# Decoder layer, float32 weights split into two float32r parts: low parts of the second-product and embedding weights by an accumulating DMA instead of a VectorE subtraction

## The chip, the cores and the metric

One Trainium2 chip, one core of it. The metric is device time in microseconds of one execution. PE is TensorE (matmuls), DVE is VectorE, ACT is ScalarE, POOL is GpSimd, SP is SyncE, which here only issues DMAs. POOL and ACT can issue DMAs too.

## What is computed

One decoder layer on 512 tokens of width 1024, in float32:

```
x = LN1(alpha*x + 0.5*SwiGLU_1(x))              # (silu(x @ Wg) * (x @ Wu)) @ W2, inner width 2816
h = x @ W_in                                    # gated delta rule (4 heads) and differential attention (4 heads)
x = LN2(alpha*x + concat(y_A, y_B) @ W_out)
x = LN3(alpha*x + 0.5*SwiGLU_2(x) + sigmoid(x @ W_pg) * (p @ W_pp))
```

## The kernel before

Precision. A product of float32 accuracy is made of three matmuls in the faster type float32r: each operand is split into a high part (the value cast to float32r) and a low part (the value minus its high part), and `mm3` (L185 to L189) adds high x high, high x low and low x high into one PSUM tile. So every weight tile that arrives from HBM goes through a split: `split` (L149) has ACT cast the raw tile to the high part `wh` and then DVE subtract it from the raw tile, which gives the low part `wl`.

Tiles. A weight unit is a tile of 128 partitions x 1024 float32 (512 KB). `load` (L153) takes a raw buffer out of a ring of four, has SP load it, and splits it. Two kinds of weights pass through it. The first kind (`ahead`, `take`) are the first-product, mixer, output and gate weights; they are read in order out of `in_wa_dram` through a ring of four `wh`/`wl` pairs. The second kind (`side`, L180) are the second-product weights of the two SwiGLU stages (W2, 22 tiles of 128 x 1024 in each) and the two tiles of W_pp, 46 tiles in all, read from `in_wb_dram`. The W2 tiles have a ring of six pairs (`w2p`).

Stages. `first_ffn`, then `mixers`, then `second_ffn`. A SwiGLU stage (`ffn`, L240) goes through the inner width in groups of 4, 6, 6 and 6 blocks of 128 columns. For each block, 24 matmuls per factor make the gate and the up factor in PSUM; `glu` has ACT apply silu, DVE multiply by the up factor, ACT cast the result to `hh` and DVE subtract to `hl`. At the end of a group come its second products: for each of four token tiles and two halves, all blocks of the group are accumulated into one PSUM tile `pb`, with the W2 tiles `wh`, `wl` as the moving operand. In the first group of `first_ffn` the four blocks are computed together, with k outermost, so that all four `glu` and all four side tiles come at once, just ahead of the second products; in every other group a block takes 48 matmuls, and its side tile comes with it.

Order. Each engine has a queue that runs in order. The order is not that of the source: when the kernel is built, a scheduler places the instructions of all engines, by costs of its own, and the ring buffers are given out in the order that it finds. So an edit can move instructions that it doesn't name. A wait on a semaphore holds up all that is queued behind it on the same engine.

Of the kernel before, what the change touches and what calls it, by code (L numbers as in the profile page):

```python
# [8 lines left out]
F32 = mybir.dt.float32  # L9
F32R = mybir.dt.float32r  # L10
BF16 = mybir.dt.bfloat16
AF = mybir.ActivationFunctionType
ALU = mybir.AluOpType
# [3 lines left out]
P = 128  # L17
# [30 lines left out]
WIDE = 2 * (512 + 2 * H)  # L48
# [32 lines left out]
class Lane:  # L81
    """A chain of steps; each step says how long it holds the tensor engine and when the next one can follow."""

# [24 lines left out]
class Layer:  # L108
# [38 lines left out]

    # ---------------------------------------------------------------- weights
    def split(self, hi, lo, src):  # L149
        self.nc.scalar.copy(hi, src)  # L150
        self.nc.vector.tensor_tensor(lo, src, hi.bitcast(F32), ALU.subtract)  # L151
# [28 lines left out]
    def side(self, pool, tag):  # L180
        r = self.load(pool, tag, self.wb[self.nb])
        self.nb += 1
        return r

# [5 lines left out]

    # ---------------------------------------------------------------- layer norm of one token tile
    def norm_natural(self, t, eps, gbt, store=None, cut=768, cuts=(0, 512, 1024)):
# [45 lines left out]

    # ---------------------------------------------------------------- SwiGLU
    def ffn(self, zone, k_outer, evac_first, natural, turn):  # L240
# [65 lines left out]

    # ---------------------------------------------------------------- start: constants and the first inputs
    def first_ffn(self):
# [75 lines left out]

    # ---------------------------------------------------------------- per-layer embedding, second SwiGLU
    def second_ffn(self):
# [63 lines left out]

    # ---------------------------------------------------------------- token mixers, output projection, LN 2
    def mixers(self):
        with ExitStack() as zone:
            self.mix_zone(zone)

    def mix_zone(self, zone):
        tc, nc = self.tc, self.nc
        act, dve, pool, pe = nc.scalar, nc.vector, nc.gpsimd, nc.tensor
# [46 lines left out]

        # ------------------------------------------------------------ projections
        def block(t, w, pq, k0, k1):
# [180 lines left out]

        # ------------------------------------------------------------ delta rule inside a chunk
        def lv4(l):  # L690
            return bc(self.LVM[:, l * P:(l + 1) * P], 1, H)
# [55 lines left out]
        def diagonal():  # L747
            """Inverts the 16 x 16 diagonal blocks of all chunks and heads, a block on each partition."""
            for b in range(8):
                r = slice(b * 16, b * 16 + 16)  # L750
# [19 lines left out]
            for b in range(8):  # L770
                r = slice(b * 16, b * 16 + 16)
# [6 lines left out]

        # ------------------------------------------------------------ attention of one query tile and head
        def attention(t, h):  # L780
# [41 lines left out]

        # ------------------------------------------------------------ delta rule over the chunks
        def to_mix(y, t, k0, tag):
# [68 lines left out]

        # ------------------------------------------------------------ output projection
        def project_out(w, half, t):
# [36 lines left out]

        # ------------------------------------------------------------ order of the work
        values_and_gates()
# [10 lines left out]
        heads = [(t, h) for t in range(NT) for h in range(H)]  # L945
# [118 lines left out]
```

## Time and profile before

| | |
|---|---|
| time, median of 3 runs | 1130.65 us (1130.26 to 1130.72) |
| span of the profiled execution, first to last instruction | 1128.3 us |
| PE busy | 1112.6 us, 99% |
| DVE busy | 521.7 us, 46% |
| ACT busy | 367.9 us, 33% |
| POOL busy | 113.7 us, 10% |
| DMA, mean over the span | 94 GB/s, 105.76 MB |

The profile is of one execution; of that execution the page prints the span but no time of its own, so the 2.35 us between its span and the median of the three runs are taken as what lies around a span. Busy time of PE counts matmuls that overlap, so that one lasts some 0.39 us in the rows and the next starts some 0.23 us after it. Times in the rows are from the start of the span.

### The profile page before, as it was taken

The numbers are of one execution on the slowest core, as the hardware profiler recorded it, in microseconds if no ns is written. First come the engines' busy times: TensorE is split into PE (matmuls) and PEld (weight loads), VectorE is DVE, ScalarE is ACT, GpSimd is POOL, SyncE is SP. The second block draws the span as 40 slices with busy tenths as digits, with TensorE's granted clock in tenths as the row PEclk, the third lists the DMA queues.
The fourth block names the chain that finished last, engine by engine and source line by source line (L and its number), as shares of the span: only waits on it lengthen the run. The fifth ranks groups of instructions, "written<-read, shape, count | busy, mean of one in ns | idle before, by whom it ended". The sixth has DMA issues, their size and how long they took to land.

```text
span 1128.3 us, 13157 instructions
## 1 busy us (share of the span) xinstructions
PE 1112.6 (99%) x5193; PEld 900.3 (80%) x5193; DVE 521.7 (46%) x822; ACT 367.9 (33%) x642; POOL 113.7 (10%) x189
## 2 busy tenths in 40 slices
PE   9999999999999999999999999999999999999996
PEld 7788888888888978778866888888888888888885
DVE  4534423432435365457674669364333324423435
ACT  4513303320331266324376533433123213303300
POOL 2000000000002202432101204000000000000013
PEclk9999999999999999999999999999999999999998
DMA  9624402420340042023110222534224214302202
GB/s 344 208 73 143 137 19 94 150 94 23 131 154 30 1 130 76 30 84 85 57 56 1 75 75 76 168 104 129 84 94 149 75 38 149 132 19 94 94 1 75
DMA packets 38062, 105.76 MB, mean 94 GB/s; under 512 B 10160, under 2 KB 12096, under 8 KB 38000
## 3 DMA queue, kind: packets, MB, share of 16 engines
q1 hardware_dynamic: 31776, 96.71, 25.8%
q0 software_dynamic: 1808, 6.04, 1.5%
q10 hardware_dynamic: 4416, 2.16, 0.7%
q8 instruction: 41, 0.67, 0.2%
q14 instruction: 21, 0.17, 0.0%
HBM read 102.41 MB, written 2.49 MB: 93 GB/s over the span
## 4 chain that ended last, share of the span: by engine, by line
PE 96%; ACT 1%; DVE 1%; POOL 1%; issue 1%; DMA 0%; POOLq 0%; SPq 0%; ACTq 0%; DVEq 0%
PE pb L187 14%; PE pb L189 14%; PE pb L188 14%; PE pc L187 7%; PE pc L188 7%; PE pc L189 7%; PE pa L188 7%; PE pa L187 7%; PE pa L189 7%; PE pc L792 2%; PE pa L725 1%; PE pa L504 1%; PE pc L811 1%; PE pa L731 1%; PE pa L229 1%
## 5 line engine op out<-in xcount | busy, mean ns | idle before, releaser
L150 ACT CAST wh<-raw 128x1024 fp32r<-128x1024 f32 (+2 forms) x181 | 183.1, 1034 | 479.4 <-PE pc L188 149.3
L151 DVE TENSOR_TENSOR wl<-raw,wh 128x1024 fp32r<-128x1024 f32 (+2 forms) x181 | 215.2, 1210 | 176.8 <-ACT wh L150 172.8
L187 PE MATMUL pb<-wh,hh 128*128 128x512 f32 (+1 forms) x358 | 138.5, 387 | 0.0
L188 PE MATMUL pb<-wl,hh 128*128 128x512 f32 (+1 forms) x358 | 138.2, 386 | 0.0
L189 PE MATMUL pb<-wh,hl 128*128 128x512 f32 (+1 forms) x358 | 138.1, 386 | 0.0
L188 PE MATMUL pa<-XL,wh 128*128 128x512 f32 x344 | 136.4, 396 | 0.0
L188 PE MATMUL pc<-XL,wh 128*128 128x512 f32 x344 | 136.2, 396 | 0.0
L187 PE MATMUL pc<-XH,wh 128*128 128x512 f32 x344 | 136.2, 396 | 0.0
L189 PE MATMUL pc<-XH,wl 128*128 128x512 f32 x344 | 136.1, 396 | 0.0
L187 PE MATMUL pa<-XH,wh 128*128 128x512 f32 x344 | 136.0, 395 | 0.1
L189 PE MATMUL pa<-XH,wl 128*128 128x512 f32 x344 | 135.6, 394 | 0.0
L187 PE MATMUL pb<-wh,XH 128*128 128x512 f32 (+2 forms) x288 | 111.0, 386 | 0.7 <-DVE RES L908 0.5
L188 PE MATMUL pb<-wl,XH 128*128 128x512 f32 (+2 forms) x288 | 107.3, 372 | 0.2 <-DVE wl L151 0.2
L189 PE MATMUL pb<-wh,XL 128*128 128x512 f32 (+2 forms) x288 | 107.2, 372 | 0.0
L250 DVE TENSOR_TENSOR sg<-sg,pc 128x512 f32<-128x512 f32 x43 | 29.5, 687 | 151.1 <-PE pc L189 150.4
L301 DVE TENSOR_TENSOR RES<-RES,pb 128x512 f32<-128x512 f32 (+1 forms) x49 | 33.1, 676 | 114.7 <-PE pb L189 114.7
L203 POOL TENSOR_SCALAR bnrs<-bnmv 128x1 f32<-128x1 f32 x12 | 6.0, 498 | 745.9 <-DVE bnmv L201 745.9
L187 PEld LDWEIGHTS pb<-wh,hh 128*128 128x128 f32 x358 | 67.3, 188 | 14.1 <-ACT hh L150 0.3
L189 PEld LDWEIGHTS pb<-wh,hl 128*128 128x128 f32 x358 | 67.3, 188 | 13.6
L188 PEld LDWEIGHTS pb<-wl,hh 128*128 128x128 f32 x358 | 67.3, 188 | 13.5
L187 PEld LDWEIGHTS pa<-XH,wh 128*128 128x128 f32 x344 | 64.6, 188 | 16.6 <-ACT wh L150 0.8
L187 PEld LDWEIGHTS pc<-XH,wh 128*128 128x128 f32 x344 | 64.7, 188 | 15.8
(233 smaller groups left out, 1483.3 us busy)
## 6 DMA issues: line engine op xcount, KB each, us to landing
raw<-in_wa_dram SPq DMA_DIRECT2D x127, 512.0 KB, 3.6
raw<-in_wb_dram SPq DMA_DIRECT2D x46, 512.0 KB, 3.5
raw<-in_wd_dram SPq DMA_DIRECT2D x4, 520.0 KB, 4.0
RES<-in_xn_dram POOLq DMA_DIRECT2D x4, 512.0 KB, 11.2
gb<-in_gb_dram POOLq DMA_DIRECT2D x8, 256.0 KB, 4.6
xr<-in_xT_dram ACTq DMA_DIRECT2D x7, 256.0 KB, 5.2
TT<-in_gb_dram POOLq DMA_DIRECT2D x4, 256.0 KB, 3.4
out_dram<-RES SPq DMA_DIRECT2D x4, 256.0 KB, 2.1
```

The source lines that it names most:

```text
L150: self.nc.scalar.copy(hi, src)
L151: self.nc.vector.tensor_tensor(lo, src, hi.bitcast(F32), ALU.subtract)
L187: pe.matmul(o, wh, xh, start=first, stop=False)
L188: pe.matmul(o, wh, xl, start=False, stop=False)
L189: pe.matmul(o, wl, xh, start=False, stop=last)
L229: self.nc.tensor.transpose(pt[:, q * P:(q + 1) * P], self.RES[t][:, c:c + P], self.ident)
L250: dve.tensor_tensor(s, s, pu, ALU.mult)
L301: dve.tensor_tensor(rj, rj, pd, ALU.add)
L504: pe.transpose(dst[:, h * P:(h + 1) * P], src[:, h, :], ident)
L725: pe.matmul(pt[:, h * P:(h + 1) * P], MP[:, 0, c, h, :], TT[:, c, h, :], start=True, stop=True)
L731: pe.matmul(pt[:, h * P:(h + 1) * P], UU[:, c, h, :], qq[:, h * P:(h + 1) * P], start=True, stop=True)
L792: pe.matmul(sc[m], DQT[r, h, t * P:(t + 1) * P], DKT[r, h, 0:n], start=True, stop=False)
```

## The change

`side` no longer goes through `load` and `split`. For each of its 46 tiles, SP still loads the raw tile and ACT still casts it to the high part. Then ACT writes minus the high part into the low tile, and POOL issues a DMA that adds the weights, read once more from HBM, onto that tile. DVE has no part in it. `load` and `split` themselves are unchanged for all other weights and activations. The rest of the diff removes comments and moves line numbers down by 8.

```
     def side(self, pool, tag):
-        r = self.load(pool, tag, self.wb[self.nb])
+        nc = self.nc
+        src = self.wb[self.nb]
+        r = self.rawp.tile([P, WIDE], F32, name=self.nm("raw"), tag="raw")[:, 0:1024]
+        hi = pool.tile([P, 1024], F32R, name=self.nm("wh"), tag=tag + "h")
+        lo = pool.tile([P, 1024], F32R, name=self.nm("wl"), tag=tag + "l")
+        nc.sync.dma_start(r, src)
+        nc.scalar.copy(hi, r)
+        nc.scalar.activation(lo, hi.bitcast(F32), AF.Copy, scale=-1.0)
+        nc.gpsimd.dma_start(lo, src, accum_op=ALU.add)
         self.nb += 1
-        return r
+        return hi, lo
```

What this moves, in the first group of `first_ffn`. The four side tiles there are, in the program before, `wh_476`/`wl_477`, `wh_482`/`wl_483`, `wh_488`/`wl_489` and `wh_494`/`wl_495`, and in the changed program `wh_476`/`wl_477`, `wh_483`/`wl_484`, `wh_490`/`wl_491` and `wh_497`/`wl_498`; they are called side tiles 0 to 3 below. `wh_410` and `wh_442` are units of the first kind; `sg`, `hh`, `hl` belong to the four `glu`.

First place: ACT, from side tile 1 to the last cast of the four `glu`. Before:

```order
L150 CAST wh_482<-raw_481 128x1024 [waits DMAHW0_49]
L150 CAST hh_450<-sg_447 128x512 [waits DVE_49]
L150 CAST hh_457<-sg_454 128x512 [waits DVE_49]
L150 CAST wh_488<-raw_487 128x1024 [waits DMAHW1_49]
L150 CAST wh_442<-raw_441 128x1024 [waits DMAHW6_49,PE_49,Activation_49]
L249 ACTIVATE sg_461<-pa_163 128x512 [waits DVE_49]
L249 ACTIVATE sg_468<-pb_165 128x512 [waits DVE_49]
L150 CAST wh_494<-raw_493 128x1024 [waits DMAHW2_49]
L150 CAST hh_464<-sg_461 128x512 [waits DVE_49]
L150 CAST hh_471<-sg_468 128x512 [waits DVE_49]
```

The same place on ACT in the changed program, from the low part of side tile 1 to that of side tile 3:

```order
L188 ACTIVATE wl_484<-wh_483 128x1024 [waits Activation_49]
L150 CAST hh_450<-sg_447 128x512 [waits DVE_49]
L150 CAST wh_442<-raw_441 128x1024 [waits DMAHW6_49,PE_49]
L150 CAST hh_457<-sg_454 128x512 [waits DVE_49]
L257 ACTIVATE sg_461<-pa_163 128x512 [waits DVE_49]
L187 CAST wh_490<-raw_489 128x1024 [waits DMAHW1_49]
L257 ACTIVATE sg_468<-pb_165 128x512 [waits DVE_49]
L188 ACTIVATE wl_491<-wh_490 128x1024 [waits Activation_49]
L150 CAST hh_464<-sg_461 128x512 [waits DVE_49]
L150 CAST hh_471<-sg_468 128x512 [waits DVE_49]
L187 CAST wh_497<-raw_496 128x1024 [waits DMAHW2_49]
L188 ACTIVATE wl_498<-wh_497 128x1024 [waits Activation_49]
```

The negated copies stand in the queue between the casts, and the cast of side tile 3 (`wh_494` before, `wh_497` now) has moved behind the last two `hh`. Ahead of this piece ACT now has, in this order, the cast `wh_476`, its negated copy, the cast `wh_483`, the cast `wh_410`, the load of the silu table and the silus `sg_447` and `sg_454`; before, these were `wh_476`, `wh_410`, the table and the two silus, and `wh_482` came behind them.

Second place: PE, the start of the second products of that group. `pb_499` before and `pb_503` now is the first half of the first token tile, `pb_513` and `pb_517` its second half, and `pa_625` and `pa_629` are the gate factor of the next block. Before, after 12 matmuls into `pa_625`:

```order
L187 MATMUL pb_499<-wh_476,hh_450 128x512 [waits Activation_49]
L188 MATMUL pb_499<-wl_477,hh_450 128x512 [waits DVE_49]
L189 MATMUL pb_499<-wh_476,hl_451 128x512 [waits DVE_49]
L187 MATMUL pb_499<-wh_482,hh_457 128x512
L188 MATMUL pb_499<-wl_483,hh_457 128x512
L189 MATMUL pb_499<-wh_482,hl_458 128x512 [waits DVE_49]
L187 MATMUL pa_625<-XH,wh_344 128x512
L188 MATMUL pa_625<-XL,wh_344 128x512
L189 MATMUL pa_625<-XH,wl_345 128x512
L187 MATMUL pa_625<-XH,wh_344 128x512
L187 MATMUL pb_499<-wh_488,hh_464 128x512 [waits Activation_49]
L188 MATMUL pb_499<-wl_489,hh_464 128x512 [waits DVE_49]
```

The same place on PE in the changed program, after 16 matmuls into `pa_629`:

```order
L195 MATMUL pb_503<-wh_476,hh_450 128x512 [waits Activation_49]
L196 MATMUL pb_503<-wl_477,hh_450 128x512 [waits DMASW5_49]
L197 MATMUL pb_503<-wh_476,hl_451 128x512 [waits DVE_49]
L195 MATMUL pb_503<-wh_483,hh_457 128x512
L196 MATMUL pb_503<-wl_484,hh_457 128x512 [waits DMASW6_49]
L197 MATMUL pb_503<-wh_483,hl_458 128x512 [waits DVE_49]
L195 MATMUL pb_517<-wh_476,hh_450 128x512 [waits DVE_49]
L195 MATMUL pb_503<-wh_490,hh_464 128x512 [waits Activation_49]
L196 MATMUL pb_517<-wl_477,hh_450 128x512
L197 MATMUL pb_517<-wh_476,hl_451 128x512
L195 MATMUL pb_517<-wh_483,hh_457 128x512
L196 MATMUL pb_517<-wl_484,hh_457 128x512
```

The group's second products start four matmuls later, the low parts are now waited for on DMA semaphores (DMASW), and the first use of side tile 2's low part has moved from the 12th matmul of the piece to the 21st, behind two more into `pb_517` and six more into `pa_629`.

Third place: PE, around the first use of side tile 3's low part. `pc_660` is the up factor of the next block. In the program before, the low part `wl_495` was first used as the 20th matmul from the start of the second products:

```order
L189 MATMUL pb_499<-wh_488,hl_465 128x512 [waits DVE_49]
L187 MATMUL pb_499<-wh_494,hh_471 128x512 [waits Activation_49]
L188 MATMUL pb_499<-wl_495,hh_471 128x512
L189 MATMUL pb_499<-wh_494,hl_472 128x512 [waits DVE_49]
L189 MATMUL pb_513<-wh_482,hl_458 128x512
```

In the changed program the same use, of `wl_498`, is the 34th, with these rows ahead of it:

```order
L195 MATMUL pb_503<-wh_497,hh_471 128x512 [waits Activation_49]
L196 MATMUL pb_517<-wl_491,hh_464 128x512
L197 MATMUL pb_517<-wh_490,hl_465 128x512
L195 MATMUL pb_517<-wh_497,hh_471 128x512
L196 MATMUL pa_629<-XL,wh_344 128x512
L197 MATMUL pa_629<-XH,wl_345 128x512
L195 MATMUL pc_660<-XH,wh_378 128x512
L196 MATMUL pc_660<-XL,wh_378 128x512
L197 MATMUL pc_660<-XH,wl_379 128x512
L195 MATMUL pc_660<-XH,wh_378 128x512
L196 MATMUL pc_660<-XL,wh_378 128x512
L196 MATMUL pb_503<-wl_498,hh_471 128x512 [waits DMASW0_49]
```

Of the 33 matmuls between the first of the second products and this one, 20 go into `pb` and 13 into `pa` and `pc`. Behind the group's second products PE has that much less of `pa` and `pc` left; from there on its order is that of before, but for one matmul that changes places with its neighbours in the first group of `second_ffn`.

Two more things follow from the rings. On SP, the raw load of side tile 1 (`raw_482`) is now given the raw buffer of side tile 0, and that of side tile 3 (`raw_496`) the buffer of side tile 1, so each waits for the ACT cast of that tile; before, they waited for subtractions of units of the first kind. On POOL, the accumulating DMAs stand behind the constant and LN 1 loads at the start, and in each stage all of them stand ahead of the stage's first layer-norm instruction.

## Rows read from the trace of the kernel before

**Rows 1.** The page: span, and busy time of PE (share, instructions).

```profile
span 1128.3 us, 13157 instructions
PE 1112.6 (99%) x5193; PEld 900.3 (80%) x5193; DVE 521.7 (46%) x822; ACT 367.9 (33%) x642; POOL 113.7 (10%) x189
```

**Rows 2.** The chain that ended last, shares of the span by engine.

```profile
PE 96%; ACT 1%; DVE 1%; POOL 1%; issue 1%; DMA 0%; POOLq 0%; SPq 0%; ACTq 0%; DVEq 0%
```

**Rows 3.** PE's waits: total us, times, longest us.

```profile
PE pb L504 <- POOL tb L543: 1.6, 1, 1.6
PE pb L189 <- DVE wl L151: 0.5, 1, 0.5
...
PE pb L188 <- DVE wl L151: 0.2, 1, 0.2
```

**Rows 4.** Stretches: length; PE, PEld, DVE, ACT, POOL busy; PEclk, DMA share, GB/s.

```profile
50.00:60.00 10.00, 10.00 (x44) 7.98 (x43) 8.71 (x11) 6.38 (x10) 0.00 (x0) 1.00 0.68 212
60.00:70.00 10.00, 10.00 (x45) 8.28 (x45) 3.89 (x5) 0.51 (x1) 0.00 (x0) 1.00 0.19 64
...
1120.00:1125.00 5.00, 0.00 (x0) 0.00 (x0) 2.52 (x4) 0.49 (x1) 3.28 (x5) 0.69 0.00 0
```

**Rows 5.** Costliest groups: subtractions of all weight units: busy, mean ns | idle before.

```profile
L151 DVE TENSOR_TENSOR wl<-raw,wh 128x1024 fp32r<-128x1024 f32 (+2 forms) x181 | 215.2, 1210 | 176.8 <-ACT wh L150 172.8
```

**Rows 6.** Raw loads of the 46 side tiles, by the tensor they read.

```profile
DMA to landing us min/median/max: 3.3/3.5/5.1
```

**Rows 7.** Timeline of ACT, first group of first_ffn: start, us, work.

```profile
41.98 1.05 ACT L150 CAST wh<-raw 128x1024 fp32r<-128x1024 f32 x1 [1.15 <-DMA raw<-in_wb_dram]
45.38 1.05 ACT L150 CAST wh<-raw 128x1024 fp32r<-128x1024 f32 x1 [2.34 <-PE pb L188]
46.44 1.28 ACT L249 ACT_TABLE_LOAD   x1
47.74 1.09 ACT L249 ACTIVATE sg<-pa 128x512 f32<-128x512 f32 x2
...
49.65 1.15 ACT L150 CAST hh<-sg 128x512 fp32r<-128x512 f32 x2
50.69 2.00 ACT L150 CAST wh<-raw 128x1024 fp32r<-128x1024 f32 x2
```

**Rows 8.** Timeline of PE, same group: next block's unit begins, then second products.

```profile
50.97 0.40 PE L187 MATMUL pa<-XH,wh 128*128 128x512 f32 x1
...
53.77 0.46 PE L187 MATMUL pb<-wh,hh 128*128 128x512 f32 x1
```

**Rows 9.** DMA issues by line: KB each, median us from issue to landing.

```profile
RES<-in_xn_dram POOLq DMA_DIRECT2D x4, 512.0 KB, 11.2
...
TT<-in_gb_dram POOLq DMA_DIRECT2D x4, 256.0 KB, 3.4
...
TT<-blocks SPq DMA_DIRECT2D x8, 16.0 KB, 2.1
```

**Rows 10.** Timeline of ACT, second group of first_ffn: its last side tile is cast second.

```profile
128.86 2.00 ACT L150 CAST wh<-raw 128x1024 fp32r<-128x1024 f32 x2 [4.03 <-PE pc L188]
130.76 0.61 ACT L150 CAST hh<-sg 128x512 fp32r<-128x512 f32 x1
134.49 1.05 ACT L150 CAST wh<-raw 128x1024 fp32r<-128x1024 f32 x1 [3.12 <-issue]
```

**Rows 11.** Timeline of PE: second products there, start and sixth block's low part.

```profile
140.07 0.39 PE L187 MATMUL pb<-wh,hh 128*128 128x512 f32 x1
...
143.71 0.39 PE L188 MATMUL pb<-wl,hh 128*128 128x512 f32 x1
```

**Rows 12.** Timeline of ACT, first group of second_ffn, as rows 10.

```profile
787.23 0.61 ACT L150 CAST hh<-sg 128x512 fp32r<-128x512 f32 x1
```

**Rows 13.** Timeline of PE there: fourth block's low part, first use.

```profile
798.86 0.39 PE L188 MATMUL pb<-wl,hh 128*128 128x512 f32 x1
```

**Rows 14.** Timeline of PE: the last matmul.

```profile
1118.45 0.28 PE L189 MATMUL pb<-wh,hl 128*128 128x256 f32 x1
```

## The prediction

> **What bounds the kernel now.** I read the page first. TensorE is busy for 1112.6 of 1128.3 us [rows 1], and the chain that ended last is TensorE to 96% [rows 2]. So a microsecond that TensorE stands still is a microsecond of the result, and work taken from another engine is worth only what TensorE now waits for it. The list of TensorE's waits says how much that is: for a subtraction that makes a low part it waits twice, 0.5 and 0.2 us, and its longest wait after the start is 1.6 us [rows 3]. VectorE's subtractions are thus hidden behind matmuls. A mean over the kernel can't show what the new low parts do, so I then went through the places where a side tile's low part is used, with the timelines of ScalarE and TensorE. They fall into two kinds: the first group of the first SwiGLU, where all four side tiles come just ahead of their use [rows 7, 8], and all later groups, where a tile comes one block (48 matmuls) ahead [rows 10 to 13].
>
> The sum is made on the profiled execution's span, 1128.3 us. The median of the runs shown is 2.35 us above it, and I carry that over unchanged.
>
> **What is removed.** 46 subtractions of 1.21 us on VectorE [rows 5], 56 us. Worth nothing: at most the 0.7 us of TensorE's waits for low parts hang on such work, and both waits lie in the mixers, where no side tile is split. I take 0.
>
> **What is added.** On ScalarE, 46 negated copies of 128x1024. The trace has none. An ACTIVATE of 512 columns took 0.60 us (two in 1.09 [rows 7]), which is a lower bound, and two of them 1.2 us an upper one; the cast of the same size took 1.05 us, 0.95 from start to start when several follow each other [rows 7], and I take that. On POOL, 46 accumulating DMAs, and 24 MB more from HBM. The DMA engines have room: 0.19 to 0.68 busy around the critical place [rows 4].
>
> **How long the accumulating DMA takes,** from POOL's issue to landing, is the unknown on which all rests; call it L. The trace has no such transfer. It moves 512 KB from HBM and reads and writes 512 KB in SBUF. Below: a plain 512 KB load lands after 3.3 to 5.1 us, median 3.5 [rows 6]. Above: POOL's own 512 KB loads took 11.2 us, four issued together at the start [rows 9]. Between: a plain 16 KB transfer takes 2.1 us [rows 9], so 496 KB more cost 1.4 us, and twice the bytes would land after 3.5 + 1.4 = 4.9 us. POOL's plain 256 KB loads at a quiet time took 3.4 us [rows 9], so POOL's queue itself adds little. I take 6 us: 4.9, and 1.1 for descriptors of a second source and for the addition; nearer to the lower rows, since the upper one is a crowd.
>
> The Trainium skill has a price too: its page "DMA: Bandwidth & Descriptors" (section "Anatomy of one DMA — SWDGE (gpsimd) path") puts a DMA from GpSimd at 2.0 us plus bytes over 436 GB/s, and "Collectives: The Full Stack" (section "The bandwidth ceiling: the fold count and why AG ≠ RS ≠ AR") says that the DMA engines' addition itself costs no cycles but doubles the read side. For 1 MB that is an estimate of 4.4 us, with which the sum below would give a stall of 2.8 us and a time near 1133.5. For a plain 512 KB the first rule gives 3.2 us where the row has 3.5; no row here shows the second.
>
> **First group of the first SwiGLU: where it costs.** I walk through ScalarE's new order. Side tile 0 is cast at 41.98 as before and done at 43.03 [rows 7]. Only then is its raw buffer free for side tile 1, which SP loads at 43.05; landing 3.5 to 5.1 us later [rows 6], I take the middle, 4.3, so its cast starts at 47.4. In before, ScalarE used this time for a unit's cast (45.38) and the silu table (46.44) [rows 7]; now both stand behind the cast of side tile 1. From 47.4 to the end of side tile 3's negated copy there lie, in the order shown, 5 casts of a tile (0.95 each), 3 negated copies (0.95, 0.95 and 1.15 with the wait for the cast just ahead), the table load (1.28), 4 silus (0.5) and 4 `hh` casts (0.53, from two in 1.15 [rows 7]): 4.75 + 3.05 + 1.28 + 2.0 + 2.1 = 13.2, so it ends at 60.6. By the same count side tile 1's copy ends at 52.6, side tile 2's at 57.5, and `hh_464` at 58.0.
>
> TensorE, if it waited for nothing, would reach these uses earlier. Its next block begins at 50.97, and 12 matmuls later, at 53.77, come the second products [rows 8]: 0.233 us per matmul. Now 16 lie ahead, so they begin at 54.70. A second-product matmul takes 0.2275 us (16 steps from 140.07 to 143.71 [rows 11]). Side tile 1's low part is the 5th, at 55.6; side tile 2's the 21st (14 of the second products and 6 units), at 59.3; side tile 3's comes after 20 second products and 13 units, at 54.70 + 4.55 + 3.03 = 62.3. They are there at 52.6 + L, 57.5 + L and 60.6 + L. With L = 6: TensorE waits at 55.6 for 58.65 (3.0 us), then at 62.3 for 63.55 (1.3 us more), then 0.1 us more at side tile 3: a stall of 60.65 + 6 - 62.3 = **4.4 us**, and in general L - 1.6. It isn't below 1.8 us however fast the DMA is, since `hh_464`, now at 58.0 behind two negated copies, is wanted at 56.3, as the 8th. After it nothing is late: the next side tile and units are wanted behind the rest of this group's second products (six accumulations of 12, 16 us), and ScalarE goes on while TensorE waits. As TensorE is the bound to the end, nothing gives the stall back.
>
> **All later groups: hidden.** In the second group, the last side tile's cast ends at 130.85, the `hh` behind it at 131.37, and ScalarE then idled 3.12 us [rows 10]; the negated copy goes there, to 132.4. The low part is wanted at 143.7, after the fifteen matmuls of five blocks [rows 11]: 11.3 us for L. In the first group of the second SwiGLU, with four blocks, the `hh` ends at 787.84 [rows 12], the copy at 788.9, and the use is at 798.86 [rows 13]: 10.0 us. With L = 6 both have over 4 us to spare. What would the cover cost if it were gone? Each of the seven groups of the second kind would stall for what L exceeds 11.3 (10.0 in one). POOL's queue holds no one up: in each stage the layer norms stand behind all these DMAs, and the last of them is issued a group's second products ahead of the first norm. The two tiles of W_pp have three gate products of 24 matmuls, at 0.23 us some 16 us, between their load and their use.
>
> **Sum.** 1128.3 - 0 + 4.4 = 1132.7 us of span; with the 2.35 us, **1135.0 us**, 0.4% slower.
>
> **Rivals.**
> *Hidden, no change that shows.* If the DMA lands about as fast as a plain one (L = 3.5), the stall is at its floor, 1.8 to 1.9 us: 1132.5. It decides at L = 3.9, where L - 1.6 is 2.26 us, 0.2% of the time, about what a measurement of this kernel can tell from no change; a raw load of side tile 1 that lands at its quickest (0.8 us sooner) moves that point to 4.7. For it: POOL's plain loads are as quick as SP's [rows 9]. Against: twice the bytes alone make 4.9. 0.20.
> *Slow addition.* If L is above 11.3, every group waits. At L = 14: 12.4 us in the first group, 2.7 in each of six and 4.0 in one, 32.6 in all: 1163. For it: POOL's 11.2 us row [rows 9], and that nothing in the trace bounds an addition. Against: that row is four transfers in a crowd. 0.12.
> *The clock falls.* TensorE's granted clock is 1.00 in every stretch of the body, but no wait there is over 1.6 us [rows 3]. After the last matmul, which ends at 1118.7 [rows 14], the clock's mean over 1120 to 1125 is 0.69 [rows 4], so it falls from full to half while TensorE stands still. A first wait of 3 us might bring that on. The 16 matmuls up to side tile 2's part, 3.65 us, would take 7.3 at half the clock: there at 66.0 instead of 63.55, and the 13 after them as many us at full clock as before (3.0) or twice that: 69.0 to 72, a stall of 6.7 to 9.7; I take 7.5, 1138. The Trainium skill states the rule in "TensorE: Matmul & The Clock Gate", section "Part 1: The HAM clock gate": an idle TensorE is throttled to 1.2 GHz and has to be busy for a while before it has 2.4 again; the end of this trace agrees with its first half. 0.11.
> *Faster.* It needs over 2.26 us from VectorE's relief, and the waits for low parts are 0.7. Also, that the low part isn't made by the DMA can be left out: TensorE's rows wait on DMA semaphores. 0.03.
>
> **Chances and range.** The forecast (stall of 2.3 to 9.7 us at the first group, nothing behind) has 0.54. Slower by over 0.2%: 0.54 + 0.12 + 0.11 = 0.77; within: 0.20; faster: 0.03. The range reaches down to a stall of 1.35 us (between the floor and what a quick raw load makes of it, 1.0), 1132, and up to L = 11.2 with 9.6 us at the first group and 1.2 at the short one, 1141.5. Outside lie the slow addition (0.12), the faster case (0.03) and a little of the hidden one.
>
> **What would show it.** In the profile after: TensorE's waits list three for the DMA that adds onto `wl`, of about 3, 1.3 and 0.1 us, all between 55 and 67 us, and none in the later groups; the DMA issues list this DMA from POOL with about 6 us to landing; VectorE's busy time is 56 us less and ScalarE's 48 more; the silu table is loaded near 49 instead of 46.4. The prediction is wrong if the addition lands in under 4 us or over 10, if the stall sits elsewhere, or if the granted clock drops after the first wait.

## The result and the profile after

The changed kernel took 1139.8 us (median of 4 runs, 1138.5 to 1141.1), beside 1130.45 us of the kernel before on the same chip: 9.35 us more, a ratio of 1.0085 with a 95% interval of [1.0071, 1.0098]. The forecast was 1135.0, 4.4 us more than before; the direction and the range held, and the size was less than half of what came.

The profiled execution has a span of 1137.2 us, 8.9 more than before. The last matmul starts at 1125.06, where before it was 1118.45 [rows 14]: 6.6 us of the 8.9 were lost before it. From there to the end of the span it is now 12.1 us, before 9.85: the other 2.3 us were lost after it. So there are two places. The last matmul now, as [rows 14]:

```profile
1125.06 0.28 PE L197 MATMUL pb<-wh,hl 128*128 128x256 f32 x1
```

The page of the kernel after, its span and busy times, the two queues that matter, and three DMA issues (as [rows 1, 6, 9]):

```profile
span 1137.2 us, 13195 instructions
PE 1115.2 (98%) x5193; PEld 900.5 (79%) x5193; DVE 471.7 (41%) x776; ACT 413.6 (36%) x688; POOL 153.6 (14%) x235
...
q1 hardware_dynamic: 31776, 96.71, 25.4%
q0 software_dynamic: 8432, 30.16, 13.3%
...
raw<-in_wb_dram SPq DMA_DIRECT2D x46, 512.0 KB, 3.7
wl<-in_wb_dram POOLq DMA_DIRECT2D x46, 512.0 KB, 6.4
RES<-in_xn_dram POOLq DMA_DIRECT2D x4, 512.0 KB, 10.9
```

VectorE has 50 us less (56 were costed), ScalarE 46 more (48). The new DMA lands after 6.4 us in the median, near the 6 us that I took. So a median that is nearly right goes with a stall that is not.

**The first place.** The waits of TensorE in the kernel after (us in total, times, longest), as [rows 3]:

```profile
PE pb L196 <- DMA wl<-in_wb_dram: 3.1, 3, 1.8
...
PE pb L195 <- ACT sg L257: 0.7, 1, 0.7
```

Those three waits, and two steps between them, on TensorE's timeline:

```profile
58.43 0.51 PE L196 MATMUL pb<-wl,hh 128*128 128x512 f32 x1 [1.82 <-DMA wl<-in_wb_dram]
...
59.45 0.62 PE L196 MATMUL pb<-wl,hh 128*128 128x512 f32 x1
59.87 0.63 PE L197 MATMUL pb<-wh,hl 128*128 128x512 f32 x1
...
65.07 0.51 PE L196 MATMUL pb<-wl,hh 128*128 128x512 f32 x1 [1.11 <-DMA wl<-in_wb_dram]
...
68.56 0.50 PE L196 MATMUL pb<-wl,hh 128*128 128x512 f32 x1 [0.20 <-DMA wl<-in_wb_dram]
```

They are the uses of side tiles 1, 2 and 3, as the prediction named them, and the list has no fourth wait for such a DMA. Eight steps from 59.45 on are 0.42 us apart, not 0.23. POOL's timeline gives the issues of side tiles 0 to 3 (the idle time ahead of each ends with ScalarE's negated copy, L188):

```profile
43.83 0.91 POOL L189 DMA_DIRECT2D wl<-in_wb_dram  x1 [13.16 <-ACT wl L188]
51.70 0.88 POOL L189 DMA_DIRECT2D wl<-in_wb_dram  x1 [6.95 <-ACT wl L188]
56.59 0.86 POOL L189 DMA_DIRECT2D wl<-in_wb_dram  x1 [4.00 <-ACT wl L188]
59.65 0.86 POOL L189 DMA_DIRECT2D wl<-in_wb_dram  x1 [2.21 <-ACT wl L188]
```

The DMA issues of the kernel after, in the stretches that hold the last three of these one by one, list their landing after 6.7, 8.4 and 8.9 us:

```profile
wl<-in_wb_dram POOLq DMA_DIRECT2D x1, 512.0 KB, 6.7
...
wl<-in_wb_dram POOLq DMA_DIRECT2D x1, 512.0 KB, 8.4
...
wl<-in_wb_dram POOLq DMA_DIRECT2D x1, 512.0 KB, 8.9
```

51.70 + 6.7, 56.59 + 8.4 and 59.65 + 8.9 are 58.4, 65.0 and 68.55, the ends of the three waits. The last of them alone sets the stall. Its use is wanted at 62.1, by the prediction's count of matmuls from 54.56, where the second products would begin here without a wait, and comes at 68.56: 6.4 us. The 3.1 us of the list are less, since 0.7 us of waiting for ScalarE, some 1.5 us of slow steps and the restart behind each wait lie outside them. Stretches of the kernel after (columns as [rows 4]) say what the DMA engines and the clock did meanwhile:

```profile
55.00:60.00 5.00, 2.79 (x10) 1.99 (x11) 2.29 (x4) 4.32 (x6) 1.21 (x2) 0.94 1.08 272
60.00:65.00 5.00, 3.96 (x12) 2.78 (x10) 0.00 (x0) 2.11 (x2) 1.28 (x2) 0.71 0.98 243
65.00:70.00 5.00, 4.73 (x19) 3.57 (x20) 1.89 (x3) 1.54 (x2) 0.08 (x1) 1.00 1.05 264
```

The DMA engines are full (shares of 0.98 to 1.08) where before they were busy for 0.68 and 0.19 [rows 4]. The granted clock's mean is 0.71 from 60 to 65, and the steps nearly twice as far apart are its lower level, 1.2 GHz, after a wait of 1.82 us.

**The second place.** The DRAIN of POOL, an instruction that the profile lists at the end of the program; first in the kernel before (instructions; min/median/max ns; first and last start):

```profile
L1060 POOLq DRAIN  x3: 40/102/2296, 1123.7 to 1128.0; - x3
```

and in the kernel after:

```profile
L1068 POOLq DRAIN  x3: 46/102/6047, 1130.3 to 1136.9; - x3
```

The longest of the three is the first one; in the kernel before it starts beside POOL's last instruction (1123.71). It took 2.30 us and ended at 1126.0, ahead of the landing of the last output DMA (issued at 1125.1, 1.7 to 2.1 us to landing). Now it takes 6.05 and ends at 1136.35, when the last output DMA had long landed. In before POOL issued 21 DMAs, now 67.

### The profile page after: what moved, and what is told of

The parts are those of the page before. It is cut to its first block, busy times and chain, and to the rows that moved or that the text cites. A ratio compares the mean times of both kernels' runs of the same rounds, so it can differ in the third digit from the quotient of the medians.

```text
span 1137.2 us, 13195 instructions
## 1 busy us (share of the span) xinstructions
PE 1115.2 (98%) x5193; PEld 900.5 (79%) x5193; DVE 471.7 (41%) x776; ACT 413.6 (36%) x688; POOL 153.6 (14%) x235
## 3 DMA queue, kind: packets, MB, share of 16 engines
q1 hardware_dynamic: 31776, 96.71, 25.4%
q0 software_dynamic: 8432, 30.16, 13.3%
## 4 chain that ended last, share of the span: by engine, by line
PE 90%; issue 3%; DMA 3%; POOL 1%; DVE 1%; ACT 1%; POOLq 0%; ACTq 0%; DVEq 0%
PE pb L195 14%; PE pb L197 14%; PE pb L196 14%; PE pc L197 7%; PE pc L196 7%; PE pc L195 7%; PE pa L196 6%; PE pa L195 6%; PE pa L197 6%; PE pc L800 2%; DMA RES<-in_xn_dram 1%; PE pa L733 1%; DMA wl<-in_wb_dram 1%; PE pa L512 1%; PE pc L819 1%
## 5 line engine op out<-in xcount | busy, mean ns | idle before, releaser
L150 ACT CAST wh<-raw 128x1024 fp32r<-128x1024 f32 (+2 forms) x135 | 138.0, 1030 | 304.4 <-PE pc L196 159.8
L151 DVE TENSOR_TENSOR wl<-raw,wh 128x1024 fp32r<-128x1024 f32 (+2 forms) x135 | 161.9, 1207 | 206.7 <-ACT wh L150 202.9
L195 PE MATMUL pb<-wh,hh 128*128 128x512 f32 (+1 forms) x358 | 138.8, 388 | 0.7 <-ACT sg L257 0.7
L195 PE MATMUL pa<-XH,wh 128*128 128x512 f32 x344 | 135.9, 395 | 0.4 <-ACT wh L150 0.4
L195 PE MATMUL pc<-XH,wh 128*128 128x512 f32 x344 | 136.1, 396 | 0.0
L189 POOL DMA_DIRECT2D wl<-in_wb_dram x46 | 39.6, 861 | 626.0 <-ACT wl L188 626.0
L195 PE MATMUL pb<-wh,XH 128*128 128x512 f32 (+2 forms) x288 | 111.0, 386 | 0.7 <-DVE RES L916 0.5
L187 ACT CAST wh<-raw 128x1024 fp32r<-128x1024 f32 x46 | 48.1, 1047 | 136.5 <-PE pb L197 111.4
L195 PEld LDWEIGHTS pb<-wh,hh 128*128 128x128 f32 x358 | 67.6, 189 | 15.2 <-ACT sg L257 1.1
L195 PEld LDWEIGHTS pa<-XH,wh 128*128 128x128 f32 x344 | 64.8, 188 | 16.7 <-ACT wh L150 0.8
```

Source lines behind the costliest of these rows:

```text
L187: nc.scalar.copy(hi, r)
L189: nc.gpsimd.dma_start(lo, src, accum_op=ALU.add)
L195: pe.matmul(o, wh, xh, start=first, stop=False)
```

## The experiments

All ratios and differences are to the kernel before, timed beside each run (medians 1129.7 to 1130.1 us). The theory after the changed kernel's profile: late landings in the first group cost 6.6 us, and a DRAIN that grows with POOL's DMAs 2.3 us.

### Which part costs what

**e1_first_old and e2_first_only** split the change in two. The subtraction stays for the first four tiles, or for all but these:

```
 def side(self, pool, tag):
     nc = self.nc
     src = self.wb[self.nb]
+    if self.nb < 4:          # e2: self.nb >= 4;  e3: self.nb < 24;  e8: self.nb != 3
+        self.nb += 1
+        return self.load(pool, tag, src)
```

> The four side tiles of the first group go back to the VectorE subtraction, the other 42 keep the accumulating DMA. Theory (late landings in the first group cost 6.6 us, a longer DRAIN of POOL at the end of the program costs 2.3 us, nothing else costs): the three waits of TensorE on wl disappear, the end still shows a DRAIN of about 5.7 us (0.59 + 0.0815 x 63 DMAs of POOL), the time is about 1132.5 us. Rival, the DMA's bytes cost a little everywhere: clearly above 1134. Rival, all of the cost is in the first group and the tail is no cost of its own: 1130.5.

Measured: 1132.09 us, +2.35 (1.0018 [1.0009, 1.0027]). TensorE waits for no DMA onto `wl`, so 42 of the 46 DMAs are hidden, and its last matmul starts at 1118.86 (before 1118.45), so 42 subtractions less give nothing back. Its DRAIN:

```profile
L1071 POOLq DRAIN  x3: 46/93/5722, 1124.1 to 1130.3; - x3
```

5.72 us, as worked out. The rival without a tail falls.

> Only the four side tiles of the first group come from the accumulating DMA, the other 42 are subtracted on VectorE. Theory: the stall of the first group is as in the changed kernel, about 6.6 us, and POOL's DRAIN at the end is 0.59 + 0.0815 x 25 = 2.6 us, off the path: about 1137 us. Together with the run above it gives back the whole 9.35 us. Rival, costs spread over all groups: under 1133.

Measured: 1136.06 us, +6.3 (1.0057 [1.004, 1.0074]), DRAIN 2.62 us. The two parts add up to 8.7 of 9.35 us; the rest lies within the intervals.

**e6_act_neg** keeps ScalarE's 46 negated copies and takes the DMA away:

```
-        nc.gpsimd.dma_start(lo, src, accum_op=ALU.add)
+        nc.vector.tensor_tensor(lo, r, lo.bitcast(F32), ALU.add)
```

> ScalarE makes the negated copy as in the changed kernel, but VectorE adds the raw tile onto it, and there is no accumulating DMA. Theory (the landing is what is late): ScalarE's order alone leaves a wait of TensorE of about 0.7 us on ScalarE, low parts of side tiles 1 to 3 are there 1.5 us behind their copies (52.9, 57.8, 60.9) ahead of their uses (55.4, 58.4, 62.1); no long DRAIN: 1131 us, within 1130.5 to 1132. Rival, ScalarE's 46 copies and its new order make the stall: 1136 or more.

Measured: 1130.16 us, +0.4 (1.0002 [0.9993, 1.0011]). TensorE's waits hold neither a `wl` nor a `sg` of the first group. So ScalarE's 46 copies cost nothing that shows. But the run doesn't keep the changed kernel's order, as its expectation took for granted: without the DMA the instructions were placed otherwise, with the silu table ahead of side tile 1 and the second products behind 12 matmuls, as before. The table on ScalarE's timeline, in the changed kernel and in e6:

```profile
48.07 1.28 ACT L257 ACT_TABLE_LOAD   x1
...
46.27 1.28 ACT L257 ACT_TABLE_LOAD   x1
```

What the new order costs by itself was not run. The changed kernel's trace shows 0.7 us of waiting for a silu (L195, above), ahead of the three waits, and since side tile 3's landing sets the end, these add nothing of their own; and it shows side tile 3's copy done at 59.35, from which the late landing counts.

### The tail

**e4_tiny46, e5_row46, e5_tiny92** add to the kernel before POOL DMAs that nothing reads; **e3_second_stage** gives the new path to 22 tiles.

```
 def side(self, pool, tag):
     r = self.load(pool, tag, self.wb[self.nb])
+    self.nc.gpsimd.dma_start(self.junk[:, self.nb % 2 * 8:self.nb % 2 * 8 + 8], self.wb[self.nb][:, 0:8])
     self.nb += 1
     ...
```

This is e4's edit; e5_row46 takes row 0 alone (`0:1`) on both sides, e5_tiny92 has two such DMAs.

> The kernel before, and behind each of the 46 subtracted side tiles one DMA from POOL of 128 x 8 values into a scratch tile that nothing reads. Theory (the DRAIN of POOL at the end grows with the number of DMAs that POOL issued): 67 DMAs as in the changed kernel, DRAIN near 6.0 us, the end 2.3 us later, no stall in the first group: 1132.8 us. Rival, the DRAIN goes by bytes or by the addition: DRAIN 2.3 us and 1130.5.

> As the run before, but each extra DMA has only one partition's 32 bytes. If the DRAIN goes by the number of DMAs: near 6.0 us, 1132.8. If it goes by descriptors or packets: about 2.3 to 2.6 us, 1130.5.

> Two extra DMAs of 128 x 8 from POOL behind each side tile, 92 in all, 113 with the 21 of before. Theory: DRAIN 0.59 + 0.0815 x 113 = 9.8 us, the end 6 us later than before: 1136.5. Rival, the DRAIN waits for a fixed thing once POOL has issued beyond some number: 6.0 us and 1132.8.

> Only the last 22 side tiles (the second SwiGLU's) come from the accumulating DMA. Theory: no stall, 43 DMAs of POOL, DRAIN 4.1 us, the end 0.3 us later: 1130.8. Rival, the DRAIN goes by what POOL issued last: 6 us and 1132.8.

Measured: 1131.87 (+1.8), 1131.63 (+1.5), 1135.89 (+5.8) and 1130.43 us (+0.3, 1.0005 [0.9995, 1.0014]), with a DRAIN of 6.05, 6.05, 9.80 and 4.09 us. The row of the one with 92 extra DMAs:

```profile
L1063 POOLq DRAIN  x3: 46/93/9804, 1123.2 to 1133.5; - x3
```

The DRAINs of seven kernels, with 21, 22, 25, 43, 63, 67 and 113 DMAs of POOL, are 2.30, 2.37, 2.62, 4.09, 5.72, 6.05 and 9.80 us. All lie on 0.59 + 0.0815 n. That line was drawn through the first and the sixth, the others came after. A DMA of 32 bytes counts as much as one of 512 KB that adds. So it goes by their number. What of a DRAIN shows in the time differs from kernel to kernel: with 6.05 us e4_tiny46 and e5_row46 cost 1.8 and 1.5, less than e1_first_old with 5.72, but the three intervals overlap.

**e10_tail** lets the changed kernel's POOL finish sooner, **e11_before_tail** is the same edit on the kernel before:

```
+        end = store is not None and t == NT - 1
+        if end:
+            dve.tensor_scalar(rs[:, 1:2], mv[:, 1:2], float(eps), None, ALU.add)
+            pool.tensor_tensor(rs[:, 0:1], rs[:, 1:2], self.mhalf[:, 0:1], ALU.pow)
+            cut = 1024          # no columns left for ScalarE and POOL
...
```

> As the changed kernel, but in the norm of the last token tile POOL does the power alone (VectorE adds eps and scales all 1024 columns), so POOL's last instruction ends some 3 us sooner. Theory (the end waits for POOL's DRAIN of 6.05 us): the DRAIN starts and ends 3 us sooner and the end is then set by the output DMAs as in the kernel before: 2.2 us less than the changed kernel, about 1137.5. Rival (the end is late for another reason, such as the output DMAs): no change, 1139.8.

> The kernel before with the same edit of the last norm. Its DRAIN of 2.3 us is not what the end waits for, so the edit is worth only what it does to the chain of the last norm: one POOL instruction of 0.8 us less, 128 columns more on VectorE twice: within 0.5 us of the kernel before, 1130 us. It would be 2 us faster if the DRAIN or POOL's last instructions set the end there too.

Measured: e10_tail 1135.76 us (+5.9, 3.4 less than the change's 9.35; about 2.2 were expected). Its DRAIN starts at 1127.2 and lasts to 1133.8, and the span ends at 1134.6, 9.1 us behind the start of its last matmul, at 1125.51, where the changed kernel has 12.1. The end follows the DRAIN. In these two kernels the DRAIN itself is longer than the line says, by 0.53 us: 6.58 here (67 DMAs) and 2.82 in e11_before_tail (21). It starts beside POOL's last instruction, which takes 0.99 us in both and 0.45 in the kernel before; that is 0.54 more, so it seems that the 0.59 holds the run of that instruction.

e11_before_tail took 1127.39 us, 2.4 less than the kernel before (0.998 [0.997, 0.9989]): it beats both kernels, and my expectation of no change was wrong. VectorE's timeline in it, and POOL's:

```profile
1119.38 0.15 DVE L205 TENSOR_SCALAR bnrs<-bnmv 128x1 f32<-128x1 f32 x1
1119.45 1.41 DVE L215 SCALAR_TENSOR_TENSOR RES<-RES,bnmv,gb 128x512 f32<-128x512 f32 x2
1120.77 1.41 DVE L224 SCALAR_TENSOR_TENSOR RES<-RES,bnrs,gb 128x512 f32<-128x512 f32 x2
```

```profile
1119.62 0.99 POOL L206 TENSOR_TENSOR bnrs<-bnrs,mhalf 128x1 f32<-128x1 f32 x1 [3.35 <-DVE bnrs L205]
```

In the kernel before, POOL's timeline ends with two products of the last 128 columns:

```profile
1123.18 0.45 POOL L213 TENSOR_TENSOR RES<-RES,gb 128x128 f32<-128x128 f32 x1 [0.61 <-ACT RES L212]
1123.71 0.45 POOL L214 TENSOR_TENSOR RES<-RES,gb 128x128 f32<-128x128 f32 x1
```

They end at 1124.2, and only then, from 1124.19 to 1125.1, SP issues the three output DMAs of this token tile: 5.7 to 6.7 us behind the start of the last matmul. In e11 SP issues the last two at 1121.55 and 1122.2, 3.7 to 4.3 us behind its last matmul (1117.88). I had looked at the DRAIN alone, and not at the stores behind POOL.

### Why the DMA lands late

**e7_plain** takes the addition from the DMA:

```
-        nc.gpsimd.dma_start(lo, src, accum_op=ALU.add)
+        nc.gpsimd.dma_start(lo, src)
```

> As the changed kernel, but POOL's DMA writes the weights plainly instead of adding them, so the low part holds the whole weight (the computation is changed there). Theory (the addition's second read crowds the DMA engines): half the reads, the landing of side tile 3 after about 5.5 us instead of 8.9, a stall of about 3 us; the DRAIN is as long, as it goes by the number of POOL's DMAs: about 1135.5 us. Rival, any 512 KB DMA issued by POOL there costs the same: 1139.8. Rival, the long DRAIN belongs to the addition: DRAIN 2.3 us and 1133.5.

Measured: 1137.7 us, +8.0 (1.0069 [1.0054, 1.0084]); it lands after 4.8 us in the median, 5.1 to 5.6 in the first group, DRAIN 6.05. So the addition costs 1.6 us of landing in the median, more in the first group (side tiles 1 to 3 after 5.3, 5.6 and 5.1 us instead of 6.7, 8.4 and 8.9), and nothing of the DRAIN. The time tells less than hoped: in this run a raw tile of the first group came later, and POOL's issues of side tiles 0 to 3 stood some 1.8 us later than in the changed kernel (45.7, 53.5, 58.3, 61.4).

**e8_third_only** uses the new path for one tile, the last of the first group, so that no accumulating DMA has another beside it.

> Only side tile 3, the last of the first group, comes from the accumulating DMA; all others are subtracted on VectorE. No other accumulating DMA then runs beside it. Its negated copy ends near 56.5, since ScalarE has three copies less ahead of it. Theory (8.9 us to landing is a crowd of accumulating DMAs on the DMA engines): it lands after 6.4 us or less, near 63, a wait of TensorE of at most 1 us: about 1131 us. Rival (a single accumulating DMA is that slow beside the raw loads there): 8.9 us, landing at 65.7, a wait of 3.4 us, about 1133.5.

Measured: 1136.52 us, +6.7 (1.0063 [1.0046, 1.008]). TensorE in this kernel waits once for such a DMA, and longer than ever:

```profile
59.44 0.39 PE L199 MATMUL pa<-XL,wh 128*128 128x512 f32 x1
64.38 0.52 PE L199 MATMUL pb<-wl,hh 128*128 128x512 f32 x1 [4.55 <-DMA wl<-in_wb_dram]
64.72 0.61 PE L200 MATMUL pb<-wh,hl 128*128 128x512 f32 x1
65.12 0.63 PE L199 MATMUL pb<-wl,hh 128*128 128x512 f32 x1
```

The DMA, issued at 56.1, landed after 8.2 us. My theory of accumulating DMAs that crowd each other falls: one is slow by itself there. Two plain loads were under way when it was issued and a third came behind it, at 62.7; the DMA issues of the same kernel, from 44 to 72, list the plain loads and it:

```profile
raw<-in_wa_dram SPq DMA_DIRECT2D x4, 512.0 KB, 4.0
raw<-in_wb_dram SPq DMA_DIRECT2D x3, 512.0 KB, 3.7
wl<-in_wb_dram POOLq DMA_DIRECT2D x1, 512.0 KB, 8.2
```

The stretches of this kernel in which it was under way (columns as [rows 4]):

```profile
55.00:60.00 5.00, 4.83 (x22) 3.61 (x20) 2.08 (x4) 1.83 (x3) 0.91 (x1) 1.00 0.86 249
60.00:65.00 5.00, 0.62 (x2) 0.58 (x3) 1.23 (x1) 1.04 (x1) 0.00 (x0) 0.97 0.89 233
```

The wait is longer than in the changed kernel although the DMA lands earlier (64.3): with the other tiles on VectorE, TensorE's order puts the use of side tile 3 at the 26th matmul of the second products, near 59.7, and not at the 34th. Here the clock is paid for too. After the wait the steps are 0.43 us apart for 7 steps, 1.4 us more than at full clock, and nothing stands behind them that would have waited anyway: 4.5 and 1.4 us make most of the 6.2 us by which its last matmul is late.

**e9_half** halves the DMA:

```
+        if self.nb < 4:
+            nc.gpsimd.dma_start(lo[:, 0:512], src[:, 0:512], accum_op=ALU.add)
+            nc.vector.tensor_tensor(lo[:, 512:1024], r[:, 512:1024], lo[:, 512:1024].bitcast(F32), ALU.add)
+        else:
+            nc.vector.tensor_tensor(lo, r, lo.bitcast(F32), ALU.add)
```

> ScalarE makes all negated copies; in the first group the accumulating DMA adds only columns 0 to 511 (256 KB), VectorE adds columns 512 to 1023 there and everything in later groups. Theory (the DMA engines' work per byte makes the landing late): the four land after about 4.5 us instead of 6.7 to 8.9, side tile 3 near 64, a stall of 1.5 to 3 us, no long DRAIN: about 1132.5. Rival (a fixed cost of such a DMA): landing still after 7 us or more, stall of 5 us, 1135 or more.

Measured: 1136.05 us, +6.2 (1.0056 [1.0042, 1.0071]); the four land after 7.6, 5.6, 6.7 and 8.2 us. The changed kernel's whole ones took 7.1, 6.7, 8.4 and 8.9, with other neighbours: half the bytes save 1.7 us at most, where the theory had them land after 4.5. This is nearer to the rival's outcome.

**f1_third_quiet and f2_all_quiet** take plain loads away beside it:

```
+        few = self.nb == 4 if tag != "u" else self.nb <= 4 and 12 <= self.na <= 15
...
+            if few:
+                nc.sync.dma_start(r[:, 0:8], src[:, 0:8])
...
```

> Only side tile 3 comes from the accumulating DMA, and five plain loads around it (four gate and up units, one side tile) read 8 columns instead of 1024, which then stand for the whole tile (the computation is changed in these). If plain loads on the same DMA engines made the single DMA land after 8.2 us: about 6 us now, landing near 62, a wait of TensorE of some 2.3 us instead of 4.5, about 1132.5 us. If a lone accumulating DMA of 512 KB is that slow by itself here: 8 us again and 1136.5.

> The changed kernel with the same five loads cut to 8 columns (the computation is changed in these; the fifth side tile is subtracted on VectorE). Plain loads as the cause: side tiles 2 and 3 overlap each other alone, so they land after some 7 us instead of 8.4 and 8.9, the stall falls by 2 us: 1137.5. Accumulating DMAs crowding each other: 8.5 us again, 1139.5.

Measured: f1 1134.95 us, +4.9 (1.0047 [1.0031, 1.0064]), landing after 7.0 us, a wait of 3.3 us. The short loads let SP issue the next units sooner, and two full loads (issued at 54.6 and 59.15, landing after 5.6 and 4.7 us) ran beside the DMA after all; so this one was only half of what I meant. f2 1138.26 us, +8.2 (1.0072 [1.0057, 1.0087]). In f2 only short loads were issued beside side tile 1; beside side tile 2 one full load, 1.7 us behind it; beside side tile 3 two full ones, and a third from 66.8 on. The DMA issues of f2, in the stretches that hold these three:

```profile
wl<-in_wb_dram POOLq DMA_DIRECT2D x1, 512.0 KB, 5.4
...
wl<-in_wb_dram POOLq DMA_DIRECT2D x1, 512.0 KB, 5.7
...
wl<-in_wb_dram POOLq DMA_DIRECT2D x1, 512.0 KB, 7.6
raw<-in_wa_dram SPq DMA_DIRECT2D x1, 512.0 KB, 5.0
```

5.4 and 5.7 us, where the changed kernel had 6.7 and 8.4. So the same DMA at the same place takes 5.4 us without full loads beside it, 5.7 with one, and 6.7 to 8.9 with two or more (6.7, 8.4 and 8.9 in the changed kernel, 7.0 in f1, 7.6 in f2, 8.2 in e8), other accumulating DMAs or none. Plain loads on the same engines are enough to make it late; how the engines share their time among the queues stays open. The kernel as a whole gained only 1.1 us from that (9.35 to 8.2), since side tile 3 sets the stall, still had company, and was issued 1.1 us later here (60.71), as one more cast had moved ahead of its copy on ScalarE.

**f3_sizes** varies the size in the later groups:

```
+        n = 0 if self.nb < 4 else (1024, 512, 128, 8)[self.nb % 4]
+        if n:
+            nc.gpsimd.dma_start(lo[:, 0:n], src[:, 0:n], accum_op=ALU.add)
+        if n < 1024:
+            nc.vector.tensor_tensor(lo[:, n:1024], r[:, n:1024], lo[:, n:1024].bitcast(F32), ALU.add)
```

> ScalarE makes all negated copies; the first group has no DMA, and from the fifth side tile on the accumulating DMA adds, in turn, 1024, 512, 128 or 8 columns, VectorE the rest. It gives the time to landing over the size in the later groups. If it goes by the bytes that the DMA engines move: about 6.2, 4.5, 3.3 and 3 us. If it is nearly fixed: 5.5 to 6.2 for all. No stall in either case; 32 such DMAs or more on top of 21 make a DRAIN near 5.4 us and a time of 1131.5 to 1132.5.

Measured: 1131.79 us, +1.7 (1.0016 [1.0007, 1.0025]). Its 42 DMAs, by size, with the median us to landing:

```profile
wl<-in_wb_dram POOLq DMA_DIRECT2D x11, 512.0 KB, 6.0
wl<-in_wb_dram POOLq DMA_DIRECT2D x11, 256.0 KB, 6.5
...
wl<-in_wb_dram POOLq DMA_DIRECT2D x10, 64.0 KB, 5.0
...
wl<-in_wb_dram POOLq DMA_DIRECT2D x10, 4.0 KB, 3.6
```

Neither theory: 4 KB land at 3.6 us, but 512 KB no later than 256 KB. Each size has its own tiles, with its own neighbours, so the order of the two largest is not a price; why half a tile saves nothing here stays open.

## Why the prediction was wrong in its size

**Right.** What bounds the kernel, and that work off VectorE is worth nothing: TensorE makes 90% of the chain that ended last still, and in e1, with 42 subtractions less, the last matmul starts no sooner. The place: three waits for `wl` of side tiles 1 to 3 that end between 58 and 69, none in the later groups, where the landings of 6.2 to 6.3 us (medians) lie under the budgets of 11.3 and 10.0; e1 shows that the 42 hidden ones cost no stall. ScalarE's chain: the negated copy took 1.06 us, the table came at 48.07. The chain was 1.2 us faster than costed: its copies ended at 51.4, 56.3 and 59.35 instead of 52.6, 57.5 and 60.6. The floor of 1.8 us, which counted on `hh_464` at 58.0, was too high for that reason: this cast was done near 56.8, and what TensorE waited for on ScalarE is 0.7 us, for a silu, which the prediction had not counted.

**The step that failed first: "How long the accumulating DMA takes"**, with one L for all tiles and the sentence that the DMA engines have room, "0.19 to 0.68 busy around the critical place". Its 6 us are 4.9 for the bytes and 1.1 for descriptors and the addition; what other transfers under way add is put at nothing, and the one row with a crowd, 11.2 us, is set aside for being one. For a quiet place 6 us was good (5.4 in f2 with no full load beside it, 6.4 in the median of all); no run shows the 1.1 by itself. At the critical place, with two or more plain loads beside it, it was 8.9. With the prediction's own formula, and these values, the stall is 8.9 - 1.6, less 1.2 for ScalarE, and 0.3 for the way from copy to issue: 6.4 us, against 6.6 in the trace.

Part of what the argument lacked is the load that the change itself puts on the engines. From the queues: POOL's queue went from 6.04 MB and 1.5% of 1128.3 us on 16 engines to 30.16 MB and 13.3% of 1137.2, so an accumulating DMA holds all engines for (151.2 - 16.9) / 46 = 2.9 us. A plain 512 KB load (524 thousand bytes) holds them for 25.4% of 1137.2 us / (96.71 / 0.524) = 1.56 us. The doubled bytes, which the prediction had used for the landing alone, give the same factor. From 50 to 70 the engines had been busy for 6.8 + 1.9 = 8.7 us; four DMAs of 2.9 (side tiles 1 to 3 and the next tile, issued at 64.22) add 11.6, which makes 20.3 in 20 us. There was no room. But such a sum doesn't give the landing: in e8, with one accumulating DMA, the shares from 50 to 70 are 0.48, 0.86, 0.89 and 0.07, 11.5 us in 20, and it landed after 8.2 us all the same. What counted is what was under way during the flight itself; without the doubled bytes (e7) the same place gave 5.1 to 5.6 us, and without the plain loads (f2) 5.4.

**The second step that failed: the sum "1128.3 - 0 + 4.4"**, which leaves the 9.85 us from the last matmul to the end as they were. Nothing was priced there, and "POOL's queue holds no one up" looked at the layer norms alone. 46 more DMAs of POOL made its DRAIN 46 x 0.0815 = 3.75 us longer; the first 1.4 were hidden behind the output DMAs, 2.3 were not. e1, e4 and e5_tiny92 show it by three doses.

**The rival "the clock falls"** had its mechanism right and was not what decided here. The clock did fall after the first wait, and the price of 0.2 us a step is in the rows. But of the changed kernel's stall it is no term of its own: the slow steps ended at 62.85, four matmuls at full clock followed, TensorE still stood 1.1 us idle until side tile 2 landed, and side tile 3's landing set the end. Nor does the length of a wait tell whether it falls: in e10_tail a longer one, of 2.89 us, left the steps at 0.23 to 0.24 us.

```profile
65.23 0.51 PE L196 MATMUL pb<-wl,hh 128*128 128x512 f32 x1 [2.89 <-DMA wl<-in_wb_dram]
65.57 0.40 PE L197 MATMUL pb<-wh,hl 128*128 128x512 f32 x1
65.81 0.40 PE L195 MATMUL pb<-wh,hh 128*128 128x512 f32 x1
```

In e8, where one late tile is all there is, the lower clock cost 1.4 us. That nothing hides it there is read from the rows; no run was made with the clock alone changed.

**The rivals "hidden" and "slow addition"** fell as argued: L was over 3.9 everywhere, and under 11.3 (5.5 to 9.3 over the 46).

## What to carry to other kernels

Where a transfer replaces work on a computing engine, list what the DMA engines have under way while the one transfer flies that someone waits for, the change's own transfers at their own weight; a share of 0.68 before is not room for a transfer that takes twice as long as a plain one, with two plain ones beside it. Read a landing time from the stretch where someone waits for it, since a median over the kernel is made of those that nobody waits for.

And look past the last matmul: who ends last there is a chain of its own, in which a queue that was used more often, or a chain of small instructions on a slow engine ahead of the last store (2.4 us in e11_before_tail), can cost more than anything that was moved in the body.

## What the runs showed of the hardware

- POOL's DRAIN at the end takes 0.59 us and 0.0815 us for each DMA that POOL issued in the whole program, whatever its size, whether it adds or not, and however long ago it landed (21 to 113 DMAs, 2.30 to 9.80 us). That holds beside a last instruction of 0.45 us; beside one of 0.99 us the DRAIN was 0.53 longer (e10_tail, e11_before_tail).
- An accumulating DMA of 512 KB holds the DMA engines 1.9 times as long as a plain load (2.9 against 1.56 us, an estimate from the queues' shares), costs POOL 0.86 us to issue, and lands after 5.4 us with no full load beside it and 6.7 to 8.9 with two or more. One of 256 KB landed after 5.6 to 8.2 us (e9_half).
- Waits of TensorE of 1.82 us (the changed kernel) and 4.55 us (e8) were followed by steps of 0.42 us at the lower clock; a wait of 2.89 us in e10_tail, and those of 1.4 and 1.2 us in e7_plain, left the granted clock at 1.00. So the length of a wait alone didn't decide it in these runs.
